# A fifth pair of gate tiles, re-opened accumulation banks and a mask inside the scan, in a hybrid attention layer on one core

## The chip, the core and the metric

The kernel runs on one core of a Trainium2 chip. The metric is the device time of one launch, in microseconds (us). Engines: PE is TensorE (matrix products; PEld its weight loads), DVE is VectorE, ACT is ScalarE, POOL is GpSimd, and SP issues nearly all DMA transfers. Every engine works through its own instruction list in order and waits on semaphores of the others. TensorE accumulates in banks of PSUM, each 128 partitions x 512 floats; ACT and DVE read them out.

## What is computed

One decoder layer on 2048 tokens (and 16 learned meta tokens ahead of them), width 1024, all in fp32:

```python
xn = rms_norm(h, norm_gain[l])
proj = xn @ w_in[l]
sb_q, sb_k, sb_v, sw_q, sw_k, sw_v, sb_z, sw_z, g_sb, g_sw = jnp.split(proj, offsets, axis=-1)
o_sb = stick_breaking_attention(...)              # 8 heads of 64, causal
o_sw = sliding_window_sink_attention(...)         # 16 query heads, 2 key heads, window 128
y_sb = (o_sb * jax.nn.silu(sb_z)) @ w_branch_sb[l]
y_sw = (o_sw * jax.nn.silu(sw_z)) @ w_branch_swa[l]
merged = jax.nn.sigmoid(g_sb) * y_sb + jax.nn.sigmoid(g_sw) * y_sw
h = h + merged @ w_out[l]
return rms_norm(h, final_norm_gain)[:, BLOCK:]
```

The four gate projections are sb_z (4 tiles of 128 columns), sw_z (8), g_sb (8) and g_sw (8): 28 gate tiles, each wanted for all tokens. The first two go through silu, x times sigmoid(x), the others through a sigmoid. Stick-breaking attention needs, along the keys of a query, a running product of 1 - sigmoid(z) over the keys before it; keys that are not strictly earlier than the query count as a factor of 1.

## The kernel before

**Precision and tiles.** Every fp32 operand is split into a high and a low part, and a product is made of three matmuls: high x high, high x low, low x high. A tile of the input projection is 128 columns of w_in against a column group of 512 tokens; over the width of 1024 that is 8 x 3 = 24 matmuls of 512 columns into one PSUM bank (`gemm`, L1181 to L1190). There are eight banks: tags g, z, t and o, two of each.

**Stages.** The four column groups are treated in two halves, groups 2 and 3 first (half 0), then 0 and 1 (half 1). In the profiled execution the stages lie thus, in us from the start of the span:

- start, to 92
- half 0: banded (sliding-window) attention, 92 to 372; stick-breaking attention, 372 to about 570; gate tiles, plain and then in 8 pairs, 580.7 to 734
- half 1: its first projections, 735 to 778; 4 pairs of gate tiles, 777.8 to 854; banded attention, 855 to 1158; stick-breaking, 1158 to 1578.6; 5 gate tiles beside the preparation of the branch outputs, 1578.6 to 1633.0
- the finish (branch projections, output projection, final norm), 1633 to 2046

Attention leaves TensorE waiting for ACT and DVE, so projection tiles are woven between its steps: `weave` takes so much of the projections per step of attention. The weaving and the order of TensorE's work are written out by hand. On ACT, DVE, SP and POOL a scheduler sets the order, but for stretches written by hand, one of which is the stretch beside the preparation of the branch outputs.

**Gate pairs** (`gate_pairs`, L1916 to L1978). For two gate tiles and two groups there are four output tiles. Instead of four full tiles, that is eight half-width products of 12 matmuls each, the kernel makes seven such products, from sums of weight halves (s1 to s4, made ahead by `pair_weights`) and sums of token halves (t1 to t4); the outputs are sums of products. Each product has a bank of its own, from the three tags g, z and t in turn (two buffers each). ACT copies the first product (a11 b11) out of PSUM, DVE adds the other products to it in seven additions, and `gate_out` applies the sigmoid (ACT) and for silu a multiplication (DVE), and stores. The names: p, u, v, w are the four sums; a11, a12, a22 and b11, b21, b22 are weight and token quarters. The weights of the next pair are loaded and summed while a pair runs. In half 0 the pairs are: pair 0 of two g_sw tiles, pairs 1 to 4 sw_z, 5 and 6 sb_z, 7 g_sw. Beside them in half 0, ACT also makes the sums of squares for the norm of the next half's tokens (`sums_ahead`, L1884: ten such squares of 128x512 while pair 1 runs).

**Half 1's other gate tiles** (`gate`, L1336). Of its 20 (sb_z, g_sb, g_sw), one stands in the first projections, three among banded attention, one ahead of stick-breaking, ten are woven into it, and five stand behind it as ten column tiles (a gate tile for one group each) of 24 matmuls in the bank tag g. After each of these ten column tiles comes one step of `pieces`, which prepares the branch outputs: it loads attention outputs and gates, multiplies them (DVE, L268), takes sums and differences of quarters (L274 to L278) and splits them (ACT L245, DVE L246), and ends with the first weights of the finish (ACT L293, DVE L295). The finish's first matmuls are L337 to L339.

**Stick-breaking rows** (`row`, L1609). For 128 queries and 512 keys: matmuls into bank z (L1643), ACT's sigmoid (L1646), a running product on DVE (`tensor_tensor_scan`, L1653), transposes on TensorE (L1668), and from these ACT (L127) and DVE (L128) split the weights for the product with v (L1700). For the blocks on the diagonal the factors that don't count must be 1. In half 0 the scan does this with a mask tile (L1651, the larger of running product x factor and the mask's value); in half 1 POOL overwrites them ahead of the scan (`affine_select`, L1648).

Of the kernel before, what the change touches and what calls it, by code (L numbers as in the profile page):

```python
# [16 lines left out]
P = 128  # L17
# [32 lines left out]
def tile_kernel(ctx, tc, x, xt, meta, metat, gain, w_in, w_sb, w_sw, w_out, sinks, fgain,  # L50
# [1178 lines left out]
    def sb_k(p):  # L1229
# [14 lines left out]
        return weights(C_SBK + p * P), use, True  # L1244

    def sb_q(p):
        def use(g, acc, ms):
            h, l = tmp(F32R), low(acc)
            evac_split(h, l, acc, 0.125)
            DMA(qd[p][g][0], h)  # L1250
            DMA(qd[p][g][1], l)
        return weights(C_SBQ + p * P), use, False
# [30 lines left out]
    def sb_v(p):  # L1283
# [50 lines left out]
        return weights(C_SBV + p * P), use, "back"  # L1334

    def gate(c0, dst, silu):  # L1336
        def use(g, acc, ms):
            e = tmp()
# [4 lines left out]
        return weights(c0), use, False  # L1343
# [234 lines left out]
    def stick(groups, bp):  # L1578
# [9 lines left out]
        mask = None  # L1588
        if groups[0]:
            mask = bp.tile([P, RW], F32, name="mask")  # L1590
            V.memset(mask[:, P:], 0.0)
            V.memset(mask[:, :P], 1.0)
            G.affine_select(out=mask[:, :P], in_=mask[:, :P], pattern=[[-1, P]], compare_op=ALU.is_ge, fill=0.0,
                            base=0, channel_multiplier=1)
# [29 lines left out]
        def row(h, g, n, j):  # L1624
# [22 lines left out]
            if n == 0 and mask is None:  # L1647
                G.affine_select(out=r[:, :P], in_=r[:, :P], pattern=[[1, P]], compare_op=ALU.is_ge,  # L1648
                                fill=1.0, base=-1, channel_multiplier=-1)
            if n == 0 and mask is not None:  # L1650
# [266 lines left out]
    def gate_pairs(ga, gb, pairs, pool, sums_x, nxt, ordered, along, between):  # L1917
# [7 lines left out]
        def product(a, b):  # L1925
            acc = ps("gzt"[next(banks) % 3])
            (wh, wl), (h, l) = a, b
            for k in range(HK):
                T.matmul(acc, lhsT=wh[:, k, :], rhs=h[:, k, :], start=k == 0, stop=False)  # L1929
                T.matmul(acc, lhsT=wh[:, k, :], rhs=l[:, k, :], start=False, stop=False)  # L1930
                T.matmul(acc, lhsT=wl[:, k, :], rhs=h[:, k, :], start=False, stop=k == HK - 1)  # L1931
            return acc

# [3 lines left out]
        def gate_out(dst, t, silu):  # L1937
            if silu:
                e = tmp()
                A.activation(e, t, AF.Sigmoid)  # L1940
                V.tensor_tensor(t, t, e, op=ALU.mult)
            else:
                A.activation(t, t, AF.Sigmoid)
            DMA(dst, t)

        for n, ((_, cdst, csilu), (_, ddst, dsilu)) in enumerate(pairs):
# [429 lines left out]
```

## Time and profile before

| what | value |
|---|---|
| time, median of 3 | 2048.16 us (2047.28 to 2048.32) |
| span of the profiled execution (no other time of it is shown) | 2045.8 us |
| busy | PE 2031.7, PEld 1706.3, DVE 1649.3, ACT 1177.5, POOL 311.4 us |
| granted clock of TensorE | full in every slice |
| moved through HBM | 198 GB/s over the span |

A row of the trace's timeline reads: start in us from the span's start, duration, engine, line, operation, output <- inputs, shapes, count, and in square brackets how long the engine was idle ahead of it and what released it. A group row of the page reads: line, engine, operation, names, shapes, count | busy us, mean ns of one | idle time of the engine ahead of these and what ended most of it. A row of the waits reads: engine, what waits <- what it waits for: us in all, times, the longest. Matmuls are pipelined: the distance from start to start is what one costs, not its duration.

### The profile page before, as it was taken

The page shows a single profiled execution, that of the slowest core. Times are in us where ns is not written, and L with a number is a line of the kernel's source. Part 1 is how long each engine was busy: PE and PEld are TensorE (multiplying, and loading weights), DVE is VectorE, ACT ScalarE, POOL GpSimd, SP SyncE. Part 2 cuts the span into 40 slices and gives each one's busy share as a digit, 9 for nine tenths or more (in the row PEclk, how much of TensorE's full clock was granted, in tenths as well). Part 3 has the DMA queues.
Part 4 walks back from the last instruction along what each step waited for, and adds up shares of the span by engine and source line. Part 5 has one row for each costly group of instructions (what it writes and reads, how often), then busy time and mean ns, then how long its engine had stood idle before and what let it go on. Part 6 is the DMA issues. An engine that isn't in the chain of part 4 may idle for free.

```text
span 2045.8 us, 31245 instructions
## 1 busy us (share of the span) xinstructions
PE 2031.7 (99%) x10375; PEld 1706.3 (83%) x10375; DVE 1649.3 (81%) x2708; ACT 1177.5 (58%) x2825; POOL 311.4 (15%) x642
## 2 busy tenths in 40 slices
PE   9999999999999999999999999999999999999998
PEld 7888888888888888888888888888888888887887
DVE  7898986877788789658887389999997788788788
ACT  6677775576755343358777366667766442335234
POOL 1233444431000000003333101000000003000000
PEclk9999999999999999999999999999999999999999
DMA  9855554865468669844344554344323779886942
GB/s 336 321 197 199 179 200 165 260 194 170 135 233 306 228 214 315 309 147 162 132 178 150 173 156 116 115 127 126 109 83 105 266 257 313 290 284 200 307 150 98
DMA packets 184065, 409.32 MB, mean 200 GB/s; under 512 B 25280, under 2 KB 29760, under 8 KB 183904
## 3 DMA queue, kind: packets, MB, share of 16 engines
q1 hardware_dynamic: 183616, 407.06, 59.0%
q8 instruction: 82, 1.34, 0.3%
q14 instruction: 79, 0.65, 0.1%
q10 hardware_dynamic: 288, 0.27, 0.0%
HBM read 256.36 MB, written 148.32 MB: 198 GB/s over the span
## 4 chain that ended last, share of the span: by engine, by line
PE 95%; ACT 2%; DVE 2%; DMA 1%; issue 1%; POOL 0%; SPq 0%; ACTq 0%; DVEq 0%; POOLq 0%
PE ps_g L1188 35%; PE ps_o L1700 6%; PE ps_z L1643 6%; PE ps_t L1668 6%; PE ps_z L1188 3%; PE ps_z L1484 3%; PE ps_o L1540 2%; PE ps_t L1518 1%; PE ps_g L1929 1%; PE ps_g L1930 1%; PE ps_g L1931 1%; PE ps_o L338 1%; PE ps_o L337 1%; PE ps_o L339 1%; PE ps_z L1929 1%; PE ps_z L1930 1%
## 5 line engine op out<-in xcount | busy, mean ns | idle before, releaser
L1188 PE MATMUL ps_g<-xh,wh 128*128 128x512 f32 x1088 | 442.3, 406 | 0.1
L1188 PE MATMUL ps_g<-xl,wh 128*128 128x512 f32 x1088 | 426.2, 392 | 0.7 <-DVE xl L2001 0.6
L1188 PE MATMUL ps_g<-xh,wl 128*128 128x512 f32 x1088 | 425.7, 391 | 0.0
L1653 DVE TENSOR_TENSOR_SCAN row<-row 128x512 f32<-128x512 f32 (+4 forms) x256 | 288.6, 1128 | 47.6 <-POOL row L1648 30.7
L1188 PEld LDWEIGHTS ps_g<-xh,wl 128*128 128x128 f32 x1088 | 204.2, 188 | 45.5 <-DVE wl L2049 0.4
L1646 ACT ACTIVATE row<-ps_z 128x512 f32<-128x512 f32 (+4 forms) x352 | 175.1, 509 | 110.3 <-PE ps_z L1643 106.3
L1188 PEld LDWEIGHTS ps_g<-xl,wh 128*128 128x128 f32 x1088 | 205.3, 189 | 34.5 <-DVE xl L2001 2.0
L1188 PEld LDWEIGHTS ps_g<-xh,wh 128*128 128x128 f32 x1088 | 204.9, 188 | 34.1 <-ACT xh L2000 0.6
L128 DVE SCALAR_TENSOR_TENSOR wtl<-ps_t,wth 128x512 fp32r<-128x512 f32 (+1 forms) x320 | 188.2, 588 | 11.3 <-ACT wth L127 11.1
L127 ACT ACTIVATE wth<-ps_t 128x512 fp32r<-128x512 f32 (+1 forms) x320 | 171.6, 536 | 41.9 <-PE ps_t L1668 39.4
L1643 PE MATMUL ps_z<-kt,q 128*128 128x512 f32 (+4 forms) x704 | 184.1, 350 | 0.7 <-ACT row L1646 0.7
L1668 PE MATMUL ps_t<-ident,row 128*128 128x128 f32 x1088 | 172.3, 273 | 1.8 <-DVE wtl L128 1.6
L1668 PEld LDWEIGHTS ps_t<-ident,row 128*128 128x128 f32 x1088 | 133.1, 140 | 35.7 <-DVE wtl L128 5.8
L1643 PEld LDWEIGHTS ps_z<-kt,q 128*128 128x128 f32 x704 | 123.8, 188 | 24.1 <-ACT row L1646 3.1
L1700 PE MATMUL ps_o<-wth,vc 128*128 128x512 f32 (+1 forms) x320 | 134.9, 422 | 0.0
L1492 ACT ACTIVATE sc<-sc,nm 128x129 f32<-128x129 f32 x256 | 100.0, 393 | 30.3 <-DVE nm L1490 29.2
L1700 PE MATMUL ps_o<-wtl,vc 128*128 128x512 f32 (+1 forms) x320 | 116.6, 364 | 0.2 <-DVE wtl L128 0.2
L1659 POOL COPY mr<-row 128x16 f32<-128x16 f32 x128 | 33.3, 263 | 382.3 <-DVE row L1653 347.7
L1477 POOL COPY sc<-skb 128x4 f32<-128x4 f32 x64 | 16.0, 256 | 458.0 <-PE ps_g L1931 304.0
L1339 ACT ACTIVATE tmp<-ps_g 128x512 f32<-128x512 f32 x63 | 37.8, 599 | 78.7 <-PE ps_g L1188 72.7
L1651 DVE TENSOR_TENSOR_SCAN row<-row,mask 128x512 f32<-128x512 f32 (+2 forms) x64 | 69.6, 1093 | 16.1 <-ACT row L1646 16.0
L1524 POOL TENSOR_SCALAR_AFFINE_SELECT pm<-ph 64x256 fp32r<-64x256 f32 x128 | 62.2, 486 | 114.7 <-ACT ph L127 110.5
(926 smaller groups left out, 4684.3 us busy)
## 6 DMA issues: line engine op xcount, KB each, us to landing
wh<-h_in_w_in SPq DMA_DIRECT2D x66, 512.0 KB, 4.0
wl<-l_in_w_in SPq DMA_DIRECT2D x66, 512.0 KB, 5.3
raw<-in_w_in SPq DMA_DIRECT2D x57, 512.0 KB, 5.6
h_in_w_in<-wh SPq DMA_DIRECT2D x50, 512.0 KB, 3.1
l_in_w_in<-wl SPq DMA_DIRECT2D x50, 512.0 KB, 4.2
q<-qd SPq DMA_DIRECT2D x128, 128.0 KB, 3.1
vc<-vd SPq DMA_DIRECT2D x48, 256.0 KB, 3.1
kd<-tmp SPq DMA_DIRECT2D x32, 256.0 KB, 3.2
```

Of the source, the lines that this page charges most:

```text
L127: A.activation(h, acc, AF.Copy, scale=scale)
L128: V.scalar_tensor_tensor(l, acc, scale, f32(h), op0=ALU.mult, op1=ALU.subtract)
L1188: T.matmul(acc, lhsT=a[:, k, :], rhs=b[:, k, :], start=k == i == 0, stop=k == KT - 1 and i == 2)
L1484: T.matmul(acc[:, a * 256:(a + 1) * 256], lhsT=lq, rhs=kk[:, 2 * kv + hl, blk * P:(blk + 2) * P], start=hl == 0, stop=hl == 1)
L1492: A.activation(sc[:, hh, :], sc[:, hh, :], AF.Exp, bias=nm[:, hh:hh + 1], accum_out=den[:, hh:hh + 1])
L1524: G.affine_select(out=pm[to, :, c], in_=full[r, :, c], pattern=[[0, 4], [sign, HB]], compare_op=ALU.is_ge, fill=0.0, base=n - 1, channel_m ...
L1643: T.matmul(z[:, :m], lhsT=qt[:, j * P:(j + 1) * P], rhs=kt[h][:, k0 + c:k0 + c + m], start=t == 0, stop=t == 1)
L1646: A.activation(r[:, c:c + m], z[:, :m], AF.Sigmoid, scale=-1.0)
L1651: V.tensor_tensor_scan(r[:, :w], r[:, :w], mask[:, :w], 1.0, op0=ALU.mult, op1=ALU.max)
L1653: V.tensor_tensor_scan(r[:, :w], r[:, :w], r[:, :w], last[j] if n else 1.0, op0=ALU.mult, op1=ALU.min)
L1668: T.transpose(tr[:, j * P:(j + 1) * P], rows_of[h, g, n - (j > i), j][:, k0:k0 + P], ident)
L1700: T.matmul(o[:, :n], lhsT=v, rhs=r, start=first and r is wh, stop=last)
```

## The change

Five things are changed:

1. Half 1 gets a fifth pair, of the last two g_sw tiles (`gts[-2:]`), behind its four of sw_z. It is made ahead of banded attention, with seven products in place of eight. So 17 ordinary gate tiles are left for after that: nine are woven into stick-breaking (ten before) and four stand behind it (five before).
2. Behind stick-breaking there are therefore eight column tiles rather than ten, with the same ten steps of `pieces`; the list `turns` says how many steps follow each.
3. In every pair but the first of a half, `opened` takes the place of the scheme with a bank for each product (which stays as `separate` for the first). A bank is now copied out by ACT after a product and the next product is added into it by TensorE, with the accumulation going on. Five of the seven products are added so: `one` takes a11 b11, s2 t2, s3 t3, a22 t4 in turn; `two` takes s1 t1 and s4 b22; only a12 b21 has its own. ACT makes four copies instead of one, DVE three additions instead of seven, and the last gate is evacuated straight from PSUM. That concerns seven pairs of half 0 and four of half 1.
4. The mask tile is made in both halves, and half 1's POOL `affine_select` (64 times) goes; its diagonal rows take the scan with the mask.
5. `gate` writes a sigmoid of a gate that is not silu back over its own input where that is a tile of SBUF.

The matmul rows of the program fall by 12, from 8884 to 8872.

Three places where the order of instructions moves. The first is on ACT, in half 0 while pair 1 runs: L1892 (after: L1887) are the squares for the next half's norm, L1877 (L1872) the high parts of the weight sums of the pair behind, L1940 (L1339) sigmoids, and L1953 (L1933) copies of products out of PSUM, the first of them that of pair 1's product 1. Before, and then after:

```order
L1892 ACTIVATE xs,ssq<-xs 128x512 x4
L1877 CAST sh<-tmp 128x512 x2
L1953 COPY tmp<-ps_z 128x512
L1940 ACTIVATE tmp<-tmp 128x512
L1877 CAST sh<-tmp 128x512
L1892 ACTIVATE xs,ssq<-xs 128x512
```

```order
L1887 ACTIVATE xs,ssq<-xs 128x512 x4
L1933 COPY tmp<-ps_z 128x512
L1872 CAST sh<-tmp 128x512
L1933 COPY tmp<-ps_z 128x512
L1339 ACTIVATE tmp<-tmp 128x512
L1887 ACTIVATE xs,ssq<-xs 128x512 x2
L1872 CAST sh<-tmp 128x512
L1933 COPY tmp<-ps_g 128x512
```

The copy has moved ahead of two casts, and still stands behind the four squares; the second copy of the same bank (after product 3) follows one cast later.

The second is on PE, at the step from product 2 to product 3 of the same pair (the last two matmuls of product 2, the first three of product 3). Before, and then after:

```order
L1930 MATMUL ps_t<-xl,wh 128x512
L1931 MATMUL ps_t<-xh,wl 128x512
L1929 MATMUL ps_g<-t2h,sh 128x512 [waits DVE_49,Activation_49]
L1930 MATMUL ps_g<-t2l,sh 128x512
```

```order
L1927 MATMUL ps_t<-xl,wh 128x512
L1928 MATMUL ps_t<-xh,wl 128x512
L1926 MATMUL ps_z<-t2h,sh 128x512 [waits Activation_49]
L1927 MATMUL ps_z<-t2l,sh 128x512
L1928 MATMUL ps_z<-t2h,sl 128x512 [waits DVE_49]
```

Product 3 goes to a bank of tag g before and back into product 1's bank, tag z, after; its first matmul waits for ACT.

The third is on ACT behind stick-breaking: L245 are the high parts of the branch outputs' pieces, L1339 the sigmoids of the gate column tiles, L293 the first weights of the finish. Before (from the sigmoid of the fifth column tile of ten on), and then after (from that of the fourth of eight on):

```order
L1339 ACTIVATE tmp<-ps_g 128x512
L245 CAST ringl<-xs 128x512 x2
L1339 ACTIVATE tmp<-ps_g 128x512
L245 CAST ringl<-xs 128x512 x3
L1339 ACTIVATE tmp<-ps_g 128x512
L245 CAST ringl<-xs 128x512 x2
L1339 ACTIVATE tmp<-ps_g 128x512
L245 CAST ringl<-xs 128x512
L245 CAST wm_77<-xs 128x512
L1339 ACTIVATE tmp<-ps_g 128x512
L293 CAST wh<-raw 128x512 x2
```

```order
L1339 ACTIVATE tmp<-ps_g 128x512
L245 CAST ringl<-xs 128x512 x2
L1339 ACTIVATE tmp<-ps_g 128x512
L245 CAST ringl<-xs 128x512 x5
L1339 ACTIVATE tmp<-ps_g 128x512
L245 CAST ringl<-xs 128x512
L245 CAST wm_77<-xs 128x512
L1339 ACTIVATE tmp<-ps_g 128x512
L293 CAST wh<-raw 128x512 x2
```

Between two sigmoids there now stand up to five casts, where there were at most three.

The diff, cut to its core:

```diff
-    def gate(c0, dst, silu):
+    def gate(c0, dst, silu, w=weights):
         def use(g, acc, ms):
-            e = tmp()
+            e = acc if spare[0] and not silu else tmp()
             A.activation(e, acc, AF.Sigmoid)
...
-        mask = None
-        if groups[0]:
-            mask = bp.tile([P, RW], F32, name="mask")
...
+        mask = bp.tile([P, RW], F32, name="mask")
...
-            if n == 0 and mask is None:
-                G.affine_select(out=r[:, :P], in_=r[:, :P], pattern=[[1, P]], compare_op=ALU.is_ge,
-                                fill=1.0, base=-1, channel_multiplier=-1)
-            if n == 0 and mask is not None:
+            if n == 0:
                 V.tensor_tensor_scan(r[:, :w], r[:, :w], mask[:, :w], 1.0, op0=ALU.mult, op1=ALU.max)
...
-        def product(a, b):
-            acc = ps("gzt"[next(banks) % 3])
+        def product(a, b, acc=None, stop=True):
+            start = acc is None
+            if start:
+                acc = ps("gzt"[next(banks) % 3])
...
+        def opened(w, cuse, duse):
+            a11, a12, a22, s1, s2, s3, s4 = w
+            one = product(a11, b11, stop=False)
+            p = copied(one)
+            other = product(a12, b21)
+            product(s2, t2, one, False)
+            u = copied(one)
+            add(p, other, p)
+            out_of(cuse, ga, p)
+            yield
+            two = product(s1, t1, stop=False)
+            w = copied(two)
+            product(s3, t3, one, False)
+            v = copied(one)
+            product(s4, b22, two)
+            add(w, w, v)
+            out_of(duse, gb, w)
+            add(u, two, u)
+            out_of(cuse, gb, u)
+            product(a22, t4, one)
+            duse(ga, one, None)
...
+            steps = opened(this, cuse, duse) if n else separate(this, cuse, duse, middle)
...
-                pairs = list(zip(swz[::2], swz[1::2]))
+                pairs = pairs_of([*(lambda w, spec=spec: gate(*spec, w) for spec in swz), *gts[-2:]])
+                del gts[-2:]
...
-            rest = 28 - FAST - PLAIN if half == 0 else 14
+            rest = 28 - FAST - PLAIN if half == 0 else 13
...
+            turns = iter((1, 2, 1, 1, 2, 1, 1, 1))
             for mk in (*gts[rest + 1:], None):
...
                 for g in groups:
                     drain(lagged(col_tile(w, g, use)))
-                    next(side)
+                    for _ in range(next(turns)):
+                        next(side)
```

94 lines of the change are left out of this document (52 added, 42 removed).

## The prediction

> **What bounds the kernel now.** I read the page's head and its chain first, then PE's waits, then the stretches that the change touches.
>
> ```profile
> span 2045.8 us, 31245 instructions
> PE 2031.7 (99%) x10375; PEld 1706.3 (83%) x10375; DVE 1649.3 (81%) x2708; ACT 1177.5 (58%) x2825; POOL 311.4 (15%) x642
> PEclk9999999999999999999999999999999999999999
> PE 95%; ACT 2%; DVE 2%; DMA 1%; issue 1%; POOL 0%; SPq 0%; ACTq 0%; DVEq 0%; POOLq 0%
> PE ps_t L1668 <- DVE wtl L128: 1.6, 5, 0.5
> ```
>
> TensorE is busy for 99% of the span, its clock reads full in every slice, and 95% of the chain is matmuls. The longest of the waits of a matmul line sums to 1.6 us. So two things count: how many matmuls go away, and whether the change makes TensorE wait where it now waits for nobody. The average of ACT (58%) does not answer the second; the order and the lateness of ACT at the places where the new waits stand do.
>
> The sum is made against the span, 2045.8 us; no other time of that execution is shown. The median, 2048.16, is 2.4 above it, and I add the sum to the median.
>
> **The fifth pair: -2.7 us.** Two gate tiles for two groups are eight products of 12 matmuls done plainly, seven in a pair. How long a product takes, from the first matmuls of the first three of half 0's pair 1:
>
> ```profile
> 599.70 0.39 PE L1929 MATMUL ps_z<-xh,wh 128*128 128x512 f32 x1
> 602.42 0.39 PE L1929 MATMUL ps_t<-xh,wh 128*128 128x512 f32 x1
> 605.14 0.42 PE L1929 MATMUL ps_g<-t2h,sh 128*128 128x512 f32 x1
> ```
>
> Start to start is 2.72 us (the 0.39 is a pipelined duration). One product fewer: 2.72 us. The other 84 matmuls change place at no cost of their own. What moves with them are two weight loads of 512 KB and four stores of 256 KB, which leave the stick and the tail and are issued by SP among half 1's pairs, ahead of what banded attention loads:
>
> ```profile
> 778.00:855.00 77.00, 77.00 (x341) 63.75 (x340) 60.02 (x97) 21.52 (x37) 0.56 (x4) 1.00 0.92 329
> ```
>
> (Length; PE, PEld, DVE, ACT and POOL busy; clock, DMA share, GB/s.) The queues are 0.92 full there and TensorE still never idles, since the weights are asked for a whole pair, 19 us, ahead: I take nothing, and up to 1 us above, what 2 MB over 329 GB/s (6 us) leave when five sixths of it hide. The 0.56 us of POOL are the mask's one select in half 0; the second mask costs as much once, beside a stage that POOL has to itself.
>
> **Opened banks, half 0, pair 1: +9.3 us.** Before, product 3 (605.14) goes to a bank of its own. Now it adds into product 1's bank, so it must wait until ACT has copied product 1 out. In-order ACT, around that copy:
>
> ```profile
> 600.65 0.63 ACT L1892 ACTIVATE xs<-xs 128x512 f32<-128x512 f32 x1 [1.20 <-DMA xs<-in_x]
> 607.94 1.05 ACT L116 CAST wh<-raw 128x1024 fp32r<-128x1024 f32 x1 [0.98 <-DMA raw<-in_w_in]
> 609.42 1.04 ACT L116 CAST wh<-raw 128x1024 fp32r<-128x1024 f32 x1
> 610.90 0.61 ACT L1892 ACTIVATE xs<-xs 128x512 f32<-128x512 f32 x1
> 613.08 0.63 ACT L1892 ACTIVATE xs<-xs 128x512 f32<-128x512 f32 x1
> 613.62 0.19 ACT L1892 ACTIVATION_READ_ACCUMULATOR xs<-xs 128x1 f32 x1
> 613.71 1.13 ACT L1877 CAST sh<-tmp 128x512 fp32r<-128x512 f32 x2
> 614.74 0.58 ACT L1953 COPY tmp<-ps_z 128x512 f32<-128x512 f32 x1
> ...
> 599.00:616.00 17.00, 16.99 (x75) 13.60 (x74) 14.26 (x23) 14.03 (x33) 0.00 (x0) 1.00 0.99 360
> ```
>
> Product 1 ends at 602.42; its copy starts at 614.74. Ahead of it ACT works through pair 0's sigmoids, pair 2's weight casts and the squares of the next half's norm: the last row, of the windows as above, has ACT busy for 14.03 of 17 us, while TensorE loses nothing. The lateness is free before because three banks rotate; this is the cover that goes. In the changed order the same instructions stand ahead of the copy, except the two casts of 613.71, which now follow it. So the copy can start at 613.8 and ends, with its 0.58 us, at 614.4; product 3 starts then instead of at 605.14: 9.3 us. Below, 7 (the squares come sooner with less in front of them); above, 10.5 (the two casts do not move).
>
> Behind this wait ACT has caught up. In pairs 2 to 7 a re-opened bank has one product (2.72 us) between its last matmul and the next use; a copy takes 0.58, so ACT may be about 2 us late. Three copies more per pair are 1.7 us of ACT in 19 us, four adds of DVE fewer. I take nothing for the steady pairs, up to 1 us each as the upper bound.
>
> [...]
>
> **TensorE's rate after the wait: +2.1 us.** The one stretch in which TensorE comes out of idleness is the start:
>
> ```profile
> 1.27 4.43 PE L91 MATMUL ps_o<-mx 128*128 128x384 f32 x13 [1.27 <-POOL mx L88]
> 5.54 0.39 PE L1188 MATMUL ps_g<-xh,wh 128*128 128x512 f32 x1
> ```
>
> Thirteen matmuls of 384 columns take 5.54 - 1.27 = 4.27 us. At the later rate, 2.72 / (12 x 512) us a column, they would take 2.21: 2.1 us lost. Bounds 0 (the start's rows have another cause) and 4 (the tail's wait, below, pays it too).
>
> [...]
>
> **Opened banks, half 1, pair 1: +1.3 us (0 to 2.5).**
>
> ```profile
> 802.28 0.39 PE L1929 MATMUL ps_g<-t2h,sh 128*128 128x512 f32 x1
> 802.39 0.63 ACT L1940 ACTIVATE tmp<-tmp 128x512 f32<-128x512 f32 x1 [0.57 <-DVE tmp L1935]
> ```
>
> The copy of product 1 stands behind pair 0's third sigmoid, which waits for DVE until 802.39. So it runs from 803.0 to 803.6; product 3 is due at 802.28. Above: another sigmoid and copy (1.2); below: the copy moves ahead.
>
> **The tail behind stick-breaking: +5.5 us (4.4 to 6.6).** Ten gate column tiles now stand beside the preparation of the branch outputs, eight after:
>
> ```profile
> 1578.60 0.39 PE L1188 MATMUL ps_g<-xh,wh 128*128 128x512 f32 x1
> 1583.88 0.69 DVE L268 TENSOR_TENSOR xs<-ringl 128x512 f32<-128x512 f32 x1 [5.90 <-DMA ringl<-ow]
> 1611.46 0.60 ACT L1339 ACTIVATE tmp<-ps_g 128x512 f32<-128x512 f32 x1 [1.49 <-PE ps_g L1188]
> 1620.05 0.62 ACT L245 CAST ringl<-xs 128x512 fp32r<-128x512 f32 x1 [1.36 <-DVE xs L268]
> 1624.62 0.62 ACT L245 CAST wm<-xs 128x512 fp32r<-128x512 f32 x1
> 1626.80 0.69 DVE L278 TENSOR_TENSOR xs<-xs 128x512 f32<-128x512 f32 x1
> 1628.34 1.13 ACT L293 CAST wh<-raw 128x512 fp32r<-128x512 f32 x2
> 1628.98 1.29 DVE L295 TENSOR_TENSOR wl<-raw,wh 128x512 fp32r<-128x512 f32 x2 [1.49 <-ACT wh L293]
> 1633.02 0.39 PE L337 MATMUL ps_o<-ringl,wh 128*128 128x512 f32 x1
> ```
>
> Ten tiles take 1633.02 - 1578.60 = 54.4 us, 5.44 each; eight would end at 1622.1. But the preparation begins when its transfer lands (1583.88, 5.3 us behind the stage's start) and its DVE and ACT chain ends at 1627.5 whatever TensorE does. With ten tiles it fits under the matmuls; with eight it sets the end. The written order makes it worse at one point: the sixth sigmoid, which frees one of the two banks for tile 8, now stands behind five casts L245, of which the last starts at 1620.05. Cast (0.62) and sigmoid (0.60) put the bank at 1621.2 where tile 8 is due at 1616.9 (1578.60 + 7 x 5.44 = 1616.7, and 0.2 for the bank's handover): TensorE idles 4.3 us, and tile 8 ends at 1626.7. The finish's own weights are then late in turn: its third matmul needs the low part that DVE makes at L295, behind L278, whose end is 1627.5; with 0.69 us for the first of two it is there at 1628.2, and the two matmuls ahead of it take 0.45. So the finish starts in effect at 1627.7, 5.3 us earlier than 1633.02 instead of the 10.9 of two tiles less: a loss of 5.5 us. The bounds are a cast and a sigmoid (1.1) either way.
>
> **The mask in the running product, half 1: -0.5 us (-1.8 to +1.8).**
>
> ```profile
> L1653 DVE TENSOR_TENSOR_SCAN row<-row 128x512 f32<-128x512 f32 (+1 forms) x224 | 258.8, 1156 | 36.8 <-POOL row L1648 30.7 <-ACT row L1646 5.1
> L1651 DVE TENSOR_TENSOR_SCAN row<-row,mask 128x512 f32<-128x512 f32 (+2 forms) x64 | 69.6, 1093 | 16.1 <-ACT row L1646 16.0
> 1158.00:1579.00 421.00, 419.16 (x2338) 351.38 (x2337) 369.97 (x469) 278.10 (x630) 37.81 (x128) 1.00 0.41 118
> ```
>
> DVE loses 30.7 us in the stage waiting for POOL's select, and a scan with the mask costs no more (1093 against 1156 ns a scan). But TensorE is idle for 1.84 of the 421 us: the most there is to win, and as much to lose when one gate tile less (10.9 us) lies over the same 370 us of DVE. I take a quarter of the gain.
>
> **Sum:** -2.7 + 9.3 + 2.1 + 1.3 + 5.5 - 0.5 = +15.0 us; 2048.2 + 15.0 = **2063.2 us**. All lower bounds at once would give 2055 and all upper ones, apart from the steady pairs, 2072; as they are independent I take about half of each way, 2059 to 2067, as the forecast's own range.
>
> **Rivals.**
> - *Transfers come sooner, and ACT is not late.* Both large terms rest on ACT or DVE work that waits for a transfer: x's tiles and weights (1.20 and 0.98 at 600.65 and 607.94), then ow's (5.90 at 1583.88). If these land sooner, both waits go: -2.7 - 0.5 (to -1.8), with half 1's 0 to 1.3: 2043.7 to 2046.3, so no slower. It decides only from 9 us at the first place and 5 at the second. Against it: a DMA share of 0.99 at the first, where the change takes no transfer away. Chance 0.14.
> - *Only the tail waits:* the scheduler's order at pair 1 holds, but ACT is on time: 2048.2 - 2.7 + 1.3 + 5.5 - 0.5 = 2051.8. Two of ACT's waits there sum to only 2.2 us, which is against it. Chance 0.12.
> - *Only half 0 waits:* the preparation hides in the tail (its inputs land as stick-breaking ends): 2048.2 - 2.7 + 9.3 + 2.1 + 1.3 - 0.5 = 2057.7. Chance 0.11.
> - *Every opened pair waits,* 0.5 to 1 us in each of eleven, through copies behind casts that themselves wait for TensorE: 5.5 to 11 more, 2069 to 2074. For it: ACT is in order and holds weight casts of 1.05 us between copies; against it: some 2 us of slack. Chance 0.07.
>
> **The numbers.** The forecast has 0.56. A measurement of this kernel tells 0.2%, 4.1 us, from no change: faster is below 2044.1, slower above 2052.3. Faster is half of the first rival, 0.08 with what lies below its price; same is the rest of it and the tail alone, 0.18; slower is 0.74. The range, 2051 to 2068, takes in all but the first and the last rival, which hold 0.2.
>
> **What would show it.** In half 0's pair 1 the first matmul of product 3 should wait some 9 us on ACT's copy, and the next dozen matmuls should start over 0.3 us apart; no later pair of that half should wait over 1 us. Half 1's pair 1 should lose about 1. Behind stick-breaking there should be one wait of 4 us on a gate's sigmoid ahead of the last column tile, and the finish should begin some 49 us after the stick's end, not 43.5. No line of POOL should release a scan any more, with half 1's stick about 11 us shorter. If the first wait is under 4 us, the place where I read ACT's lateness was wrong; if pairs 2 to 7 wait, it was the slack.

## The result and the profile after

The changed kernel takes 2074.06 us (median of 4, 2072.85 to 2076.45) against 2048.24 us for the kernel before, run beside it: a ratio of 1.0131, 95% interval 1.0117 to 1.0145. It is 25.8 us slower. The direction was forecast, the size was not: 15 us were predicted, and 2074 lies outside the range.

The head of the changed kernel's page, the engines' shares of its chain, and the two longest lines of PE's waits:

```profile
span 2070.8 us, 31086 instructions
PE 2038.2 (98%) x10363; PEld 1706.8 (82%) x10363; DVE 1633.2 (79%) x2681; ACT 1197.6 (58%) x2863; POOL 292.3 (14%) x579
...
PE 79%; DVE 9%; DMA 6%; ACT 4%; issue 2%; SPq 1%; POOL 0%; DVEq 0%; ACTq 0%; POOLq 0%
...
PE ps_z L1926 <- ACT tmp L1933: 10.7, 3, 8.3
PE ps_g L1188 <- ACT tmp L1339: 4.4, 2, 3.6
```

TensorE's share of the chain has fallen from 95% to 79%. DVE, DMA and ACT now hold 19% of it, after 5% before. That says where the chain runs, not how much time was lost there. The two waits are the opened bank (L1926 is a product, L1933 ACT's copy) and the column tile behind the late sigmoid, both named in the prediction.

Where the 25.0 us between the two spans lie shows when the stages are cut at the first matmul of each (us; the half 1 pairs are four before, five after). "Work moved" is the time of the matmuls that came or went, "lost" is what is left of the difference. The profiled execution took 2072.85 us, the shortest of the four, so the table accounts for 25.0 us and not for all of the 25.8:

| stage | before | after | difference | of it work moved | lost |
|---|---|---|---|---|---|
| gate pairs, half 0 | 153.16 | 164.23 | +11.1 | 0 | 11.1 |
| gate pairs, half 1 | 76.16 | 103.31 | +27.1 | +19.0 | 8.1 |
| banded attention, half 1 | 326.19 | 326.15 | 0.0 | 0 | 0 |
| stick-breaking, half 1 | 398.45 | 390.98 | -7.5 | -10.9 | 3.4 |
| behind it, to the finish | 54.42 | 48.48 | -5.9 | -10.9 | 4.9 |

The work moved comes to -2.7, the product saved. The last column adds to 27.5; 25.0 is left with the 0.2 us of the other stages. Half 0's wait, in PE's timeline (first the last matmul of product 2), in ACT's, and in the windows (length; PE, PEld, DVE, ACT, POOL busy; clock, DMA share, GB/s):

```profile
605.42 0.39 PE L1928 MATMUL ps_t<-xh,wl 128*128 128x512 f32 x1
614.10 0.80 PE L1926 MATMUL ps_z<-t2h,sh 128*128 128x512 f32 x1 [8.29 <-ACT tmp L1933]
614.70 0.63 PE L1927 MATMUL ps_z<-t2l,sh 128*128 128x512 f32 x1
615.12 0.63 PE L1928 MATMUL ps_z<-t2h,sl 128*128 128x512 f32 x1
```

```profile
608.09 1.04 ACT L116 CAST wh<-raw 128x1024 fp32r<-128x1024 f32 x1 [0.86 <-DMA raw<-in_w_in]
612.87 0.61 ACT L1887 ACTIVATE xs<-xs 128x512 f32<-128x512 f32 x1
613.49 0.56 ACT L1933 COPY tmp<-ps_z 128x512 f32<-128x512 f32 x1
```

```profile
597.00:616.00 19.00, 10.71 (x44) 8.46 (x43) 15.82 (x25) 13.62 (x33) 0.00 (x0) 0.84 0.98 362
616.00:640.00 24.00, 24.00 (x99) 19.64 (x98) 12.26 (x23) 16.61 (x30) 0.00 (x0) 0.91 0.70 261
```

The copy behind the squares starts at 613.49 (predicted: 613.8) and product 3 at 614.10 (predicted: 614.4). A wait is counted here from start to start, less the 0.23 us that a matmul takes: 614.10 - 605.42 - 0.23 = 8.45 us. Behind it the matmuls start 0.43 us apart, and the clock, 1.00 in the windows of these pairs before the change, reads 0.84 and 0.91.

### The profile page after: what moved, and what is told of

Read it like the earlier page. It is cut to its first block, busy times and chain, and to the rows that moved or that the text cites. A ratio compares the mean times of both kernels' runs of the same rounds, so it can differ in the third digit from the quotient of the medians.

```text
span 2070.8 us, 31086 instructions
## 1 busy us (share of the span) xinstructions
PE 2038.2 (98%) x10363; PEld 1706.8 (82%) x10363; DVE 1633.2 (79%) x2681; ACT 1197.6 (58%) x2863; POOL 292.3 (14%) x579
## 4 chain that ended last, share of the span: by engine, by line
PE 79%; DVE 9%; DMA 6%; ACT 4%; issue 2%; SPq 1%; POOL 0%; DVEq 0%; ACTq 0%; POOLq 0%
PE ps_g L1188 29%; PE ps_o L1695 6%; PE ps_z L1641 6%; PE ps_t L1663 6%; PE ps_z L1484 3%; PE ps_o L1540 2%; PE ps_z L1926 2%; PE ps_z L1928 1%; PE ps_z L1927 1%; PE ps_t L1518 1%; PE ps_o L339 1%; PE ps_o L338 1%; PE ps_o L337 1%; DVE row L1648 1%; PE ps_z L1188 1%
## 5 line engine op out<-in xcount | busy, mean ns | idle before, releaser
L1188 PE MATMUL ps_g<-xh,wh 128*128 128x512 f32 x1056 | 429.3, 407 | 5.0 <-ACT tmp L1339 4.4
L1188 PE MATMUL ps_g<-xl,wh 128*128 128x512 f32 x1056 | 413.5, 392 | 0.7 <-DVE xl L2036 0.6
L1188 PE MATMUL ps_g<-xh,wl 128*128 128x512 f32 x1056 | 413.3, 391 | 0.0
L1188 PEld LDWEIGHTS ps_g<-xh,wl 128*128 128x128 f32 x1056 | 198.3, 188 | 44.0 <-DVE wl L120 0.3
L1188 PEld LDWEIGHTS ps_g<-xh,wh 128*128 128x128 f32 x1056 | 198.9, 188 | 38.7 <-ACT tmp L1339 5.2
L1188 PEld LDWEIGHTS ps_g<-xl,wh 128*128 128x128 f32 x1056 | 199.3, 189 | 33.5 <-DVE xl L2036 1.9
L1648 DVE TENSOR_TENSOR_SCAN row<-row 128x528 f32<-128x528 f32 (+1 forms) x192 | 210.6, 1097 | 17.8 <-ACT row L1644 17.4
L1646 DVE TENSOR_TENSOR_SCAN row<-row,mask 128x512 f32<-128x512 f32 (+4 forms) x128 | 147.3, 1155 | 40.0 <-ACT row L1644 39.3
L1477 POOL COPY sc<-skb 128x4 f32<-128x4 f32 x64 | 16.1, 257 | 495.6 <-PE ps_z L1928 342.2
L1524 POOL TENSOR_SCALAR_AFFINE_SELECT pm<-pl 64x256 fp32r<-64x256 f32 x128 | 73.9, 577 | 37.4 <-DVE pl L128 31.8
```

What stands on the lines that cost most here:

```text
L1188: T.matmul(acc, lhsT=a[:, k, :], rhs=b[:, k, :], start=k == i == 0, stop=k == KT - 1 and i == 2)
L1524: G.affine_select(out=pm[to, :, c], in_=full[r, :, c], pattern=[[0, 4], [sign, HB]], compare_op=ALU.is_ge, fill=0.0, base=n - 1, channel_m ...
L1646: V.tensor_tensor_scan(r[:, :w], r[:, :w], mask[:, :w], 1.0, op0=ALU.mult, op1=ALU.max)
L1648: V.tensor_tensor_scan(r[:, :w], r[:, :w], r[:, :w], last[j] if n else 1.0, op0=ALU.mult, op1=ALU.min)
```

## The experiments

Each run is read by stage, since the whole times of most variants of the changed kernel lie within each other's intervals. A stage varies by itself, too: half 0's first wait was 8.5 to 10.1 us in the nine profiles that leave that place as it is, and half 1's five opened pairs took 99.1 to 104.6 us in the nine that change nothing in them. Each stage length below is of one profile. `open_only`, `pair5_only` and `from_banded` were made from the changed kernel and keep its item 5, the sigmoid written over its input; no run tests that item alone.

**The parts by themselves.** `mask_only`:

```diff
-            if n == 0 and mask is None:
-                G.affine_select(out=r[:, :P], ...)
-            if n == 0 and mask is not None:
+            if n == 0:                      # mask made in both halves
```

> The kernel before with the mask in half 1's scan as its only edit (POOL's 64 selects gone). In the changed kernel half 1's stick-breaking is 7.5 us shorter where a gate tile less should make it 10.9 shorter, so 3.4 us were lost there. Theory 'cover' (one gate tile less over the same DVE work loses them): this kernel is within 1 us of before, 2047 to 2049, and its stick as long as before. Rival 'mask' (the scan with the mask is dearer on DVE than POOL's select was, 1221 ns a scan against 1156): the stick gets 3 us longer, 2051.

Measured: 2047.36 us, ratio 0.9999 (0.999 to 1.0009); half 1's stick 398.55 us. The mask does nothing to the time, though DVE's 30.7 us of waiting for POOL are gone: the rival falls. "Cover" (TensorE's work that lies over the other engines' work in a stage) is tested by `pair5_only` and `ten_woven`, which take such work out and put it back.

`open_only` (`opened` as in the change, no fifth pair, selects kept, ten gate tiles woven and five behind):

> The kernel before with the opened banks as its only edit (pairs 1 to 7 of half 0, 1 to 3 of half 1; no fifth pair, POOL's selects kept). Theory 'late copies': all that the pairs lose comes from the copies, so half 0's pairs lose 11 us and half 1's some 6 to 8: 2065 to 2067. Rival 'traffic of the fifth pair' (half 1's 8.1 us come from the loads and stores that moved there): half 1's pairs lose under 2 us, 2060.

Measured: 2064.76 us, 1.0087 (1.0072 to 1.0102). Half 0's pairs take 163.44 us, 10.3 more, half 1's four pairs 82.42, 6.3 more; everything else is as before. The opened banks lose in both halves without the fifth pair and its traffic.

`pair5_only` (a bank for each product in every pair, selects kept):

```diff
-            steps = opened(this, cuse, duse) if n else separate(this, cuse, duse, middle)
+            steps = opened(this, cuse, duse) if False else separate(this, cuse, duse, (lambda: None) if n else middle)
...
```

> The kernel before with the fifth pair as its only edit: every product in a bank of its own, POOL's selects kept, eight column tiles behind the stick with the same turns. Theory 'late copies': no wait in the pairs; -2.7 for the product, +5 in the tail, and under 'cover' +3.4 in the stick: 2051 to 2054. Rival 'traffic of the fifth pair': half 1's pairs lose their 8 us here, 2059 to 2062.

Measured: 2056.12 us, 1.0044 (1.0028 to 1.0061). Half 1's five pairs take 95.20 us, 19.04 more than four: seven products and not 0.1 us beside. So the traffic of the fifth pair costs nothing in the pairs. But the stick is only 6.4 us shorter and the tail 4.3 instead of 10.9 each: the fifth pair alone is a loss, 2 us above the range of its theory, which had allowed 3.4 and 5 us for what is 4.4 and 6.6.

`first_plain`:

```diff
-            steps = opened(this, cuse, duse) if n else ...
+            steps = opened(this, cuse, duse) if n > (ga == 2) else ...
```

> The changed kernel, but half 0's pair 1 has a bank for each product as before (pairs 2 to 7 stay opened). Theory 'ACT is late only at pair 1': the 8.5 us wait and the slow matmuls behind it go, 11 us less than the changed kernel, 2063. Rival 'the first opened pair pays': the wait moves to pair 2, 2070 to 2074. The tail's 3.7 us wait stays in both.

Measured: 2065.9 us, 1.0092 (1.0077 to 1.0107); half 0's pairs 158.62 us. Half of the 11 us went; the other half moved to pair 2:

```profile
PE ps_t L1926 <- ACT tmp L1933: 3.2, 1, 3.2
```

Both theories were half right: with pair 1 left alone, the copy is still 3.2 us late at pair 2, where the prediction saw nothing.

**Half 1's pairs: what makes the copies late.** Cut at each pair's first matmul, the 8.1 us lie in pair 0 (1.8), pair 1 (2.3), pair 2 (0.3) and pair 3 (3.7); pair 4 loses nothing. Pair 0 keeps a bank for each product. Its waits are for the halves of its own weight sums, and why these come later than before was not followed:

```profile
PE ps_g L1926 <- ACT sh L1869: 0.7, 1, 0.7
PE ps_g L1928 <- DVE sl L1874: 0.4, 1, 0.4
```

The longest wait, in pair 3, looks like this on DVE, ACT and PE:

```profile
848.49 0.69 DVE L1903 TENSOR_TENSOR xs<-xs 128x512 f32<-128x512 f32 x1 [5.22 <-DMA xs<-in_w_out]
854.67 0.69 DVE L1904 TENSOR_TENSOR xs<-xs 128x512 f32<-128x512 f32 x1 [3.68 <-issue]
855.88 0.69 DVE L1937 TENSOR_TENSOR tmp<-ps_g,tmp 128x512 f32<-128x512 f32 x1
```

```profile
856.66 0.63 ACT L1339 ACTIVATE tmp<-tmp 128x512 f32<-128x512 f32 x1 [4.50 <-DVE tmp L1937]
857.20 0.58 ACT L1339 ACTIVATE tmp<-ps_z 128x512 f32<-128x512 f32 x1
857.67 0.58 ACT L1933 COPY tmp<-ps_z 128x512 f32<-128x512 f32 x1
```

```profile
858.30 0.50 PE L1926 MATMUL ps_z<-t2h,sh 128*128 128x512 f32 x1 [1.83 <-ACT tmp L1933]
```

DVE stands at the sums of w_out (L1903 to L1906). The row names no releaser for its second wait; in the trace a load of w_out issued at 846.54 lands at 854.59, just ahead of it. Pair 2's addition is queued behind it, ACT's sigmoid behind that, pair 3's copy behind the sigmoid.

`sums_behind` (`output_weight_sums` drained behind the pairs instead of one step in each) and `own_tiles` (the copies w and v in the three tiles of `short`):

> The changed kernel, with the sums of the output weights (four loads of w_out and four DVE operations per pair) taken out of half 1's pairs and done behind the last of them. In the changed kernel DVE stands in those pairs behind loads of w_out (5.22 and 3.68 us in pair 3), with a pair's addition queued behind, ACT's sigmoid behind that and the copy behind the sigmoid. Theory 'DVE behind w_out': the 2.0 us wait of pair 3 and its slow matmuls go, half 1's five pairs take 98 to 100 us instead of 103.3, the rest is unchanged: 2069 to 2071. Rival 'slots of the copies' (a copy needs a tile that a store still reads): under 1 us, 2073.

> The changed kernel, with the copies w and v of half 1's pairs in three tiles of their own, not in the ring of nine that also holds sums, sigmoids and stores. Theory 'slots of the copies': the waits of a copy for a store of a gate (1.40 and 0.53 us in pair 1) go, with TensorE's 1.25 us there: half 1's pairs take 101 to 102 us instead of 103.3, 2072. Rival 'DVE behind w_out': under 0.5 us, and pair 3's 2 us wait stays.

Measured: 2073.24 us, 1.0126 (1.0112 to 1.014), pairs 101.03; and 2073.4 us, 1.0129 (1.0116 to 1.0143), pairs 102.51. Neither tells anything: both lie within the spread of 99.1 to 104.6. In the first the scheduler had put DVE's sums back among the pairs, with 5.32 and 3.54 us of waiting at the same two lines. In the second the wait at the copy w was gone, and pair 3's had grown to 3.0 us.

`no_sums`:

```diff
-            V.tensor_tensor(b11, b12, b11, op=ALU.subtract)
-            ... (the four sums; loads and stores of w_out stay)
```

> The changed kernel, with the four DVE operations on w_out in each of half 1's pairs left out (the loads and stores of w_out stay, unsummed, so the output weights' sums are left out of the result). Moving that work behind the pairs left DVE's order as it was and its waits in place, so that run did not test it. Theory 'DVE behind w_out': the 1.9 to 2.2 us wait of pair 3's first copy goes, and of the 8.1 us that half 1's pairs lose 3 to 5 go: 98 to 100 us for the five pairs, 2069 to 2071. Rival 'ACT's order' (the copy stands behind two sigmoids whatever DVE does): under 1 us.

Measured: 2074.84 us, 1.0134 (1.0119 to 1.0149), pairs 103.95. The wait of pair 3 did go, but one of 6.1 us came in pair 1, behind a weight load on DVE:

```profile
809.14 0.69 DVE L1857 TENSOR_TENSOR tmp<-raw 128x512 f32<-128x512 f32 x1 [6.38 <-DMA raw<-in_w_in]
```

So taking DVE's own work on w_out away did not shorten the pairs: they lose 8.75 us without it, within the spread. What DVE then waits for is a transfer. `no_wout`:

```diff
-            b11, b12, b22, b21 = (ring_x() for _ in range(4))
-            ... (16 loads, the sums, 16 stores of 256 KB)
+            (one load and one store in all; every sum reads that tile)
```

> The changed kernel, with all work on the output weights' sums left out of half 1's pairs (16 loads and 16 stores of 256 KB but one each, and the DVE operations); the sums are left out of the result. ACT's order stays as it is. Leaving out only the DVE operations moved the wait from pair 3 to pair 1 (6.1 us), where DVE waited 6.4 us for a weight load. Theory 'transfers pace DVE and ACT': with 8 MB fewer the five pairs take 95.2 to 97.5 us instead of 103.3: 2066 to 2068. Rival 'ACT's order' (the copy stands behind the sigmoids of the pair before): 100 us or more.

Measured: 2068.85 us, 1.0105 (1.0088 to 1.0121), 0.9 above the range of its theory; the five pairs take 95.55 us, as it said, 0.35 over the 95.20 of separate banks. Of PE's waits in the pairs one line is left, half 0's first wait. Behind it the five pairs in `no_wout`, in the changed kernel and in `pair5_only`, in the windows:

```profile
PE ps_z L1923 <- ACT tmp L1930: 9.4, 1, 9.4
```

```profile
789.27:884.82 95.55, 95.50 (x421) 78.75 (x420) 54.27 (x86) 33.94 (x59) 0.00 (x0) 1.00 0.66 226
789.38:892.69 103.31, 98.60 (x422) 79.42 (x420) 63.94 (x103) 34.78 (x61) 0.00 (x0) 0.98 0.83 284
778.32:873.52 95.20, 95.20 (x422) 78.85 (x420) 69.85 (x112) 27.09 (x46) 0.00 (x0) 1.00 0.86 310
```

With a DMA share of 0.66 the opened pairs of half 1 do not wait. In the changed kernel it is 0.83. With separate banks it is 0.86, and TensorE loses nothing either. So w_out's transfers make DVE and ACT late there, and the opened banks hand that lateness to TensorE. Whether the fullness of the queues or the order in which SP issues into them delays a load was not separated.

**Half 0's first wait.** `small_squares`:

```diff
-                A.activation(t, t, AF.Square, accum_out=ssq[:, f, i:i + 1])
+                A.activation(t[:, :64], t[:, :64], AF.Square, accum_out=ssq[:, f, i:i + 1])
```

> The changed kernel, with the 16 squares beside half 0's pairs made on 64 columns in place of 512 (the squares of the other columns are left out of the norm of half 1's tokens). ACT's instructions stand in the same order up to the copy. Theory 'ACT has too much in front of the copy': the eight squares between product 2's end and the copy, 0.63 us each now, shrink to 0.25 to 0.3, so half 0's 8.5 us wait falls by 2.5 to 4 us, to 4.5 to 6: 2070 to 2071.5. Rival 'ACT is late because transfers are' (its waits for x and for weights pace it): under 1 us.

Measured: 2071.79 us, 1.0118 (1.0103 to 1.0133), wait 8.5 us as before. ACT with less to do waited longer for transfers, and the copy came at the same time. The windows are the stretch from product 1's end to the copy, in the changed kernel and here; ACT is busy for 9.70 and 7.21 us of it:

```profile
602.93:613.49 10.56, 2.88 (x13) 2.06 (x11) 9.26 (x15) 9.70 (x25) 0.00 (x0) 0.83 0.96 341
602.86:613.49 10.63, 2.89 (x13) 2.06 (x11) 8.77 (x14) 7.21 (x24) 0.00 (x0) 0.76 0.96 330
```

```profile
608.53 1.04 ACT L116 CAST wh<-raw 128x1024 fp32r<-128x1024 f32 x1 [1.45 <-DMA raw<-in_w_in]
613.49 0.56 ACT L1933 COPY tmp<-ps_z 128x512 f32<-128x512 f32 x1
```

`light_x` (the loads of x cut to 64 columns as well), `pool_casts` (`hsplit[0] = n > 1 or ga != 2` around pair 2's `pair_weights`, so that POOL casts them) and `both_away` (both):

> The changed kernel, with the 16 loads of x for the squares beside half 0's pairs cut to 64 of 512 columns (0.5 MB instead of 4) and the squares with them; the other columns are left out of the norm of half 1's tokens. Shrinking the squares alone left the 8.5 us wait as it was. Theory 'transfers pace ACT' (ACT waits for x and for the weights of pair 2, with the queues 0.94 to 1.03 full around the wait): the weights land earlier and the wait falls to under 4 us: 2065 to 2069. Rival 'something else ahead of the copy' (the casts and sigmoids themselves): still over 6 us, 2071 to 2073.

> The changed kernel, with the two weight casts of half 0's pair 2 made on POOL instead of ACT (POOL is idle there); no transfer is taken away, and the rest of ACT's order up to the copy stays. Cutting x's transfers took 2 of the 8.5 us of half 0's wait and left the weights of pair 2 asked for at 602.6 us, with ACT's casts of them (1.5 and 0.2 us of waiting, 1.05 each) ahead of the copy. Theory 'the casts hold ACT until the weights land': without them the wait falls to 2.5 to 5.5 us: 2067 to 2071. Rival 'x's transfers pace ACT' (the squares ahead of the copy wait for x as long): still over 7 us, 2072 to 2074.

> The changed kernel, with both edits at once: the loads of x and their squares cut to 64 columns (the rest is left out of the norm of half 1's tokens) and the casts of pair 2's weights on POOL. Each alone left the copy of product 1 at 611.5 to 613.1 us: with the casts gone ACT waits for x, with x cut it waits for the weights. Theory 'two transfers, each enough': together the copy comes right behind pair 0's last sigmoid, at 608.5 to 609.5 us, and the wait is 3 to 4.5 us: 2064 to 2067. Rival 'a third thing ahead of the copy': the wait stays over 6 us, 2069 or more.

Measured: 2071.05 us, 1.0111 (1.0096 to 1.0126), wait 6.6; 2071.48, 1.0116 (1.01 to 1.0133), wait 8.8; 2071.51, 1.0114 (1.0098 to 1.0131), wait 5.8. What ACT waits for ahead of the copy, in the three in turn:

```profile
606.75 1.04 ACT L116 CAST wh<-raw 128x1024 fp32r<-128x1024 f32 x1 [1.54 <-DMA raw<-in_w_in]
611.51 0.56 ACT L1933 COPY tmp<-ps_z 128x512 f32<-128x512 f32 x1
```

```profile
610.07 0.63 ACT L1887 ACTIVATE xs<-xs 128x512 f32<-128x512 f32 x1 [1.72 <-DMA xs<-in_x]
613.07 0.57 ACT L1933 COPY tmp<-ps_z 128x512 f32<-128x512 f32 x1
```

```profile
608.45 0.26 ACT L1887 ACTIVATE xs<-xs 128x64 f32<-128x64 f32 x1 [1.42 <-DMA xs<-in_x]
610.22 0.56 ACT L1933 COPY tmp<-ps_z 128x512 f32<-128x512 f32 x1
```

Take one obstacle away and the next sets the time: with x light, the weights; with the casts gone, x; with both, the small loads of x again, and two sigmoids. The first two went to their rivals (over 6 and over 7 us); the last fell between its theory (3 to 4.5 us) and its rival (over 6). No single cause was found for the 8.5 us. In the changed kernel ACT works for 9.7 of the 10.6 us and waits for one transfer, 0.86 us; with the squares cut, waits for x and the weights grow to 3.4. Work and transfers take each other's place there, so taking one away leaves the other.

**The stick and what stands behind it.** `ten_woven`:

```diff
-            rest = 28 - FAST - PLAIN if half == 0 else 13
+            rest = 28 - FAST - PLAIN if half == 0 else 14
-            turns = iter((1, 2, 1, 1, 2, 1, 1, 1))
+            turns = iter((2, 2, 2, 2, 1, 1))
```

> The changed kernel, with ten gate tiles woven into half 1's stick again and three behind it (six column tiles with 2, 2, 2, 2, 1, 1 steps). Theory 'cover' with 'the preparation sets the end': the stick takes 398.5 us again (7.5 more) and the tail, though it has 10.9 us of matmuls less, still 47 to 50: 2079 to 2082. Rival 'TensorE sets both': the tile only changes place and the sum of the two stays within 2 us, 2072 to 2076.

`tail_turns`:

```diff
-            turns = iter((1, 2, 1, 1, 2, 1, 1, 1))
+            turns = iter((1, 2, 2, 1, 1, 1, 1, 1))
```

> The changed kernel, with the steps of the preparation behind stick-breaking dealt out as 1, 2, 2, 1, 1, 1, 1, 1 instead of 1, 2, 1, 1, 2, 1, 1, 1, so that the fifth sigmoid and not the sixth stands behind five casts. Theory 'the preparation sets the end': TensorE waits at another column tile, but the finish starts within 1 us of where it did, 48.5 to 50.1 us behind the stick's end: 2073 to 2075. Rival 'the order of ACT sets it': the finish starts 2 to 4 us earlier.

Measured: 2080.45 us, 1.0163 (1.0146 to 1.018), and 2075.65, 1.0132 (1.0116 to 1.0147). The windows of half 1's stick before, after, with the fifth pair alone (`pair5_only`) and with ten woven again:

```profile
1180.15:1578.60 398.45, 396.61 (x2239) 332.71 (x2237) 367.26 (x464) 275.16 (x625) 37.81 (x128) 1.00 0.38 111
```

```profile
1218.84:1609.82 390.98, 388.44 (x2191) 323.47 (x2190) 366.97 (x464) 275.23 (x623) 18.20 (x64) 1.00 0.37 110
```

```profile
1199.66:1591.68 392.02, 389.13 (x2190) 322.80 (x2189) 366.44 (x464) 275.44 (x623) 38.28 (x128) 1.00 0.37 109
```

```profile
1217.06:1615.51 398.45, 396.58 (x2238) 332.88 (x2237) 368.12 (x464) 275.70 (x625) 18.28 (x64) 1.00 0.37 111
```

DVE's busy time (367.26 us in the first row) stays at 366 to 368 us; the stage is what shrinks around it, and it shrinks by 6.4 us (7.5 with the mask, so the mask is worth 1.0 us there) when 10.9 us of matmuls leave. With ten woven it takes 398.45 us again, to the hundredth. TensorE's idle time hardly shows the loss: 1.84 us in the first row, 2.54 in the second. A matmul is drawn 0.39 us long while the next can start 0.23 us behind it, so a short wait between two starts counts as busy. The tail with six column tiles (32.6 us of matmuls) takes 47.77 us, with eight 48.48, and with eight dealt out otherwise 50.89, within the 48.5 to 51.2 of all runs with eight tiles (0.8 above what its theory gave). So the preparation sets its end, and another order of the sigmoids did not bring the finish forward. Its DVE chain in the changed kernel, first and last:

```profile
1614.56 0.69 DVE L268 TENSOR_TENSOR xs<-ringl 128x512 f32<-128x512 f32 x1 [5.37 <-DMA ringl<-ow]
1658.29 0.69 DVE L278 TENSOR_TENSOR xs<-xs 128x512 f32<-128x512 f32 x1
```

That is 43.7 us from first to last, against 42.9 before (1583.88 to 1626.80), with eight column tiles and with ten.

**Taking the tiles from elsewhere.** `from_banded` (mask, five pairs with separate banks, ten woven, ten column tiles behind):

```diff
-            few = 2 if m else 3
+            few = 2 if m else 1
-SR = (1.05, 1.05)
+SR = (1.05, 1.18)
```

> The kernel before with the mask, a fifth pair with a bank for each product, and the two gate tiles of the pair taken out of banded attention (one there instead of three, its ratio of weaving raised from 1.05 to 1.18), so that ten stay in the stick and ten column tiles behind it. Theory 'cover' (the fifth pair is worth its 2.7 us where the tiles are taken from a stage that TensorE sets, and DVE is 78% busy in banded attention against 94% in the stick): banded attention 21.8 us shorter, pairs 19 us longer, nothing else: 2044.5 to 2046. Rival 'any stage needs its tiles': banded attention gets less than 17 us shorter, 2048 to 2052.

Measured: 2063.14 us, 1.0074 (1.0061 to 1.0088). That is more than the theory (up to 2046) and the rival (up to 2052) gave. Banded attention became 4.2 us shorter, not 21.8, in a profile of the slowest of the five executions (2066.95):

```profile
PE ps_z L1641 <- DMA q<-qd: 7.6, 1, 7.6
PE ps_z L1484 <- DVE q L1465: 4.2, 6, 1.9
```

DVE is 67% busy over the whole of that stage (the 78% of the expectation holds for its middle), and TensorE still waits once the tiles are gone, for a transfer at its end and for DVE within: its idle time there rises from 0.25 us to 13.0. An average share does not say what a stage can spare. Only one ratio of weaving was run, so a better one is not ruled out.

`after_again` (the changed kernel once more):

> The changed kernel once more, for the slow matmuls behind a wait. In its first profile a wait of 2.2 us was followed by ten slow ones and a wait of 4.0 us by none; with the fifth pair alone a wait of 3.9 us was followed by a dozen. [...] Rival 'the wait's place decides': the same waits as in the first profile. The time is 2074 either way.

Measured: 2075.17 us, one run; its rows are used in the last section. No variant pointed to a version that beats the kernel before: opening a bank saves no matmul, and the fifth pair's 2.7 us were less than the cover lost in each of the places that its tiles were taken from.

## Why the prediction was right or wrong, step by step

- **The fifth pair, -2.7:** right as matmuls (19.04 us for seven products, `pair5_only`). Zero for its traffic was right too.
- **Half 0's pair 1, +9.3:** 8.45 us, and 8.5 to 10.1 in the profiles that leave the place alone. The place, the size and the instructions ahead of the copy held. That ACT's work alone sets the copy's time did not: with its squares cut, waits for transfers took the work's place.
- **The rate after the wait, +2.1:** 2.6 (the stage's 11.1 less 8.45).
- **Half 1's pairs, +1.3: wrong, 8.1.** The step that failed is "I take nothing for the steady pairs, up to 1 us each as the upper bound." Pairs 2 to 4 lost 4.0 us, 3.7 of them in pair 3; pair 1, the only one in the sum, lost 2.3, and pair 0, for which the sum has no term, 1.8. The 2 us of slack of a copy were enough in half 0's pairs 2 to 7, but the lateness was measured only for ACT's own instructions. In half 1 w_out's transfers make DVE late, its additions and the sigmoids behind it, and so the copies; before, three banks in rotation hid it. The prediction quoted the DMA share of 0.92 and concluded only that TensorE does not idle. The size is one execution's: in the nine profiles with these pairs unchanged the loss is 3.9 to 9.4 us, 6.1 in the middle. Half 0's pairs 2 to 7 waited for no copy, so the last rival, each of eleven pairs, did not happen either; that its time (2069 to 2074) did is chance.
- **The tail, +5.5:** 4.9, by the preparation as described. This is the lowest of the 13 profiles with eight column tiles; the others give 6.3 to 7.7. In two of those the tail's clock reads below the 1.00 of the changed kernel: 0.66 in the 4 us behind the wait in `after_again`, and 0.97 over the whole tail in `pair5_only`.
- **The stick, -0.5: wrong, +3.4.** The step that failed is the bound: TensorE's idle time of 1.84 us was taken as the most to lose. What can be lost is set by the work of the other engines that the removed matmuls covered: 10.9 us of cover went, and 3.4 us (4.4 without the mask) came back as later starts. The mask gained nothing with ten tiles woven (398.45 us without it, 398.55 and 398.45 with it) and 1.0 us with nine. The 0.56 us of POOL that the prediction took for the mask's select is four copies of sink keys (L1477); the select took 0.62 us, so its price was about right.

Two mis-sized terms, 6.8 and 3.9 us, less 0.9 by which half 0 and the tail came out smaller, make the 9.8 us between the 15.0 of the sum and the 24.8 of the table. The other microsecond to 25.8 is the 0.2 of the other stages and the distance of the profiled execution from the median. The first rival (transfers come sooner, nothing waits) fell: neither wait went.

## What to carry to other kernels

When a change makes the busiest engine wait for another one's queue, follow that queue back to the transfers, not only through its own instructions; the rotation of buffers that was given up here had hidden the lateness of all of it (half 1's five pairs take 95.20 us with it and 103.31 without). Idle time of the busiest engine does not bound what is lost when its work leaves a stage (here 1.84 us idle, 3.4 lost); that is set by the other engines' work in that stage (here DVE's 366 to 368 us), and is measured by taking one tile out. A stage with a chain that cannot start before a transfer lands (here 43 us on DVE) gives back next to nothing for matmuls taken out beyond the chain's own length: with six column tiles in place of eight the tail took 47.8 us, against 48.5 to 51.2, where 10.9 us of matmuls had gone.

## What the runs showed of the hardware

The slow matmuls behind a wait were expected; when they come was not. In the changed kernel's pairs they start 0.43 us apart instead of 0.23: 13 of them behind half 0's wait of 8.45 us and eight behind half 1's longest, which cost 2.9 and 1.7 us against a start every 0.23 us. Behind the 5.8 us of `both_away` in half 0's pair 1 the clock reads 0.54 from 610 to 615 us. Of the shorter waits some were followed by them and some not, at the same place in the same program. The windows behind half 1's wait in the changed kernel, 2.2 us with the whole distance from start to start, then behind its tail's wait of 4.0 us, and last behind that same wait in the repeat:

```profile
858.30:862.00 3.70, 3.70 (x10) 2.96 (x11) 3.70 (x8) 0.00 (x0) 0.00 (x0) 0.60 0.95 324
```

```profile
1653.00:1657.00 4.00, 4.00 (x19) 3.27 (x19) 3.25 (x6) 1.41 (x3) 0.00 (x0) 1.00 0.35 131
```

```profile
1654.00:1658.00 4.00, 3.53 (x10) 2.83 (x11) 3.25 (x6) 1.08 (x3) 0.00 (x0) 0.66 0.32 120
```

The clock reads 0.60 after a wait of 2.2 us, 1.00 after one of 4.0, and 0.66 after the same one in the repeat. In these rows neither the wait's place nor its length alone says which clock follows, so the rival of `after_again` falls. In the changed kernel's trace the clock stands at 0.50 from 609.89 to 620.13 (10.24 us) and from 859.06 to 862.47 (3.41 us). The 3.41 us with half 1's wait and those behind them, then two stretches of that length that share the tail's wait, in the changed kernel:

```profile
855.65:859.06 3.41, 1.58 (x7) 1.02 (x6) 3.41 (x7) 1.59 (x3) 0.00 (x0) 1.00 0.82 271
859.06:862.47 3.41, 3.41 (x9) 2.64 (x9) 3.41 (x6) 0.00 (x0) 0.00 (x0) 0.50 0.99 327
1647.54:1650.95 3.41, 1.61 (x8) 0.99 (x6) 2.69 (x6) 1.24 (x2) 0.00 (x0) 1.00 0.21 77
1650.95:1654.37 3.42, 1.65 (x7) 1.39 (x8) 2.70 (x5) 1.11 (x2) 0.00 (x0) 1.00 0.21 77
```

TensorE is idle for 1.83 us of the first, and the clock reads 0.50 behind it; of the last two it is idle for 1.80 and 1.77 us, and the clock reads 1.00 there and in the 3.41 us behind them. What decides between the two is not shown. For a sum, a wait of 2 to 4 us in these rows cost 1.4 to 1.7 us more (an estimate, from 4.00 us at a clock of 0.66 and 3.41 us at 0.50) or nothing, and no row of the kernel before shows which it will be.
